# Feed-forward up-projections by seven products of sums of quarters, down-projections in three parts

## The chip, the cores and the metric

The kernel runs on one core of a Trainium2 chip. The metric is the device time of one execution in microseconds. The kernel before takes 1202.05 us (median of three runs, 1201.83 to 1202.29). The engines are TensorE (PE for its matmuls, PEld for its weight loads), VectorE (DVE), ScalarE (ACT), GpSimd (POOL) and SyncE (SP, which issues nearly all loads).

## The reference

One decoder layer over 512 tokens of width 1024, all in float32:

```python
x = x + 0.5 * swiglu(rmsnorm(x, ffn1_norm), ffn1_wgu, ffn1_wdown)
h = rmsnorm(x, mix_norm); z = h @ w_in         # q, k, v, conv, gates
a = sliding_window_attention(q, k, v, sinks) @ attn_proj
c = silu(layernorm(conv(ca * sigmoid(cb)))) @ conv_proj
x = x + (sigmoid(ga) * a + sigmoid(gb) * c) @ w_out
x = x + 0.5 * swiglu(rmsnorm(x, ffn2_norm), ffn2_wgu, ffn2_wdown)
x = x + sigmoid(rmsnorm(x, ple_gate_norm) @ ple_gate_w) * rmsnorm(p @ ple_proj, ple_norm)
# swiglu(h, wgu, wd):  g, u = split(h @ wgu);  (silu(g) * u) @ wd      with 2816 features
# rmsnorm(x, g):       x * rsqrt(mean(x * x) + eps) * g
```

Nearly all of the arithmetic is in the matrix products: the two feed-forwards have 3 x 1024 x 2816 weights each, the rest some ten products of 1024 x 1024.

## The kernel before

Activations lie transposed in SBUF, features on the 128 partitions and the 512 tokens along the free dimension, so x is eight tiles of 128x512 (`x[k]`, KD = 8). A float32 product is made of three matmuls in the reduced-precision type fp32r. Every operand is split into a high part (`hi`, ACT, a copy that rounds) and a low part (`lo`, DVE, source minus high). `mm3` (line 702) then adds lo x hi, hi x hi and hi x lo into one PSUM bank. A matmul has a 128x128 block of weights as its stationary operand and 512 tokens as its moving one.

Weights come in pieces of 128x1024 floats (512 KB): `piece` (line 690) loads one (SP), and splits it. There are three buffers for raw pieces, three for high and three for low parts (`SLOTS`, line 641: raw, hi, lo), 53 tiles of 128x512 for everything else (class a), four tiles four times as wide (class o), two of class k that hold the keys, and the eight PSUM banks (ps).

A feed-forward is the function `ffn` (line 852). Its 22 tiles of features are taken one by one: `products` multiplies the gate and the up part of a tile, 2 x 8 x 3 = 48 matmuls of 512 columns, into two banks. `gated` multiplies both by the norm's factor `rb` (one number per token, spread over the partitions), takes silu of the gate (ACT), the product, and its split. When all 22 are there, eight down-projections follow, each over all 22 tiles (66 matmuls) into one bank, and one DVE instruction adds half of it to `x[o]`. `after(o)` (`next_norm`) makes the next stage's split input and adds its squares on POOL. The factor of a norm is made from sums of columns (`mean_rstd`: eight matmuls of one column, then Newton steps on four numbers per partition) and spread by `spread` (two matmuls with diagonal matrices).

The program isn't written in the order in which it runs. `record` notes all operations; `simulate` lays them on the engines with a table of costs (`costs`), giving each a latest start (`deadlines`), and the order found becomes each engine's queue. TensorE's groups of matmuls may be taken out of order within a window of 8 groups (`WINDOW`). Operations given to `nc.flex` may be put on DVE or on POOL. `ORDER` (line 40) lists the steps of the middle of the layer (convolution, attention, gates), whose steps are not touched otherwise.

All instructions of the program have the line 1348 in the profile, so they are told apart by the names of their tiles: `f_g`, `f_u` and `f_d` are the gate, up and down products of both feed-forwards, `raw_wgu`, `whi_wgu` and `wlo_wgu` a piece of up-projection weights and its halves, `f_gs`, `f_us`, `f_a` the activations, `kvb` the keys' and values' product, `cz` the convolution on DVE, `y` on POOL, `pg` the last gate.

Of the kernel before, what the change touches and what calls it, by code (L numbers as in the profile page):

```python
# [9 lines left out]
F32 = mybir.dt.float32  # L10
F32R = mybir.dt.float32r
I32 = mybir.dt.int32
# [7 lines left out]
D = 1024  # L20
KD = D // P
FF = 2816
KF = KF2 = FF // P
NH = 16
NKV = 2
HD = 64
# [11 lines left out]


ORDER = """  # L40
K0 a0 a2 a1 Q0 A0 b2 b1 b0 a3 A1 E0 E1 b3 A2 E2 a4 V0 A3 a5 E3 V1 b4 Q1 V2 b5
A4 V3 A5 a7 A6 g5 h7 E5 A7 E6 E4 V6 g3 E7 g0 a6 V5 V4 g4 g6 b6 V7 h1 g2 h4 b7
g1 p0 p2 g7 L0 p3 p6 p4 h3 p7 p5 p1 e0 h5 h6 e1 h0 h2
"""
POOLCH = (0, 2, 4)
WARM = 9
MARGIN = 0.0

CAPS = {"cz": 2, "ct": 4}
# [175 lines left out]
class Program:  # L225
    def __init__(self):
        self.ops, self.groups, self.tiles = [], [], []
        self.cur = None
# [15 lines left out]
    def add(self, eng, what, a, k):  # L244
        op = Op()
        op.flex = eng == "FLEX"
        eng = "DVE" if op.flex else eng
        op.i, op.eng, op.home, op.what, op.a, op.k = len(self.ops), eng, eng, what, a, k
        out = [a[0]] if isinstance(a[0], V) else []
        if isinstance(k.get("accum_out"), V):  # L250
            out.append(k["accum_out"])
        if what == "tensor_tensor_reduce":
            out.append(a[7])
        ins = [v for v in a[1:] if isinstance(v, V) and not any(v is o for o in out)]
        ins += [v for n, v in k.items() if isinstance(v, V) and n != "accum_out"]
        op.writes, op.reads = out, ins
        op.preds, op.succs = {}, []
        op.start = op.end = None
        op.done = False
        for vs, w in ((ins, False), (out, True)):  # L260
            for v in vs:
                p0, p1, m, _ = v.region()
                keep = []
                for e in v.vt.log:
                    o, q0, q1, mm, ww = e
                    if (w or ww) and o is not op and p0 <= q1 and q0 <= p1 and m & mm:

                        op.preds[o] = op.preds.get(o, False) or ww
                        if w and p0 <= q0 and q1 <= p1 and not (mm & ~m):
                            continue  # L270
                    keep.append(e)
                v.vt.log = keep
                keep.append((op, p0, p1, m, w))
        for o in op.preds:
            o.succs.append(op)
        op.outs = [v.vt for v in out]
        op.vts = list(dict.fromkeys(v.vt for v in out + ins))
        for vt in op.vts:
            vt.left += 1
        self.costs(op, "POOL" if op.flex else None)  # L280
        op.group = None
        if eng == "PE":
# [101 lines left out]
        op.ls = ls  # L384


WINDOW = 8


def simulate(prog, slots):  # L390
# [253 lines left out]
def record():  # L644
# [19 lines left out]
    ones = nc.tile("ones", [P, P], F32, "c")  # L664
    nc.vector.memset(ones, 1.0)

    nc.scalar.activation(small("table", 1), ones[:, 0:1], AF.Silu)
# [34 lines left out]
    def mm3(ps, w, x, start, stop, first=1):  # L702

        nc.tensor.matmul(ps, w[first], x[0], start=start, stop=False)
        nc.tensor.matmul(ps, w[1 - first], x[0], start=False, stop=False)
        nc.tensor.matmul(ps, w[0], x[1], start=False, stop=stop)

    def part(w, s):
        return w[0][:, s], w[1][:, s]
# [40 lines left out]
    def spread(name, rr):  # L750
# [21 lines left out]
        nc.scalar.copy(rb, ps)  # L772
        return rb

    class SumSq:
        def __init__(self, name):
            self.name, self.accs, self.n = name, [], 0
# [23 lines left out]
    g_all = nc.tile("g_all", [P, 8, KD], F32, "c")  # L801
    nc.scalar.dma_start(g_all, Dram("gains"))
    g_ffn1, g_mix, g_ffn2, g_gate, g_ple, dwb, lng, lnb = (g_all[:, i] for i in range(8))

    x, h = [], []
    ss = SumSq("n1")
# [45 lines left out]
    def ffn(tag, wgu, wdown, h, ss, after, cuts, late, KF):  # L852

        rb = None
        acts = []
        ups = []
        quads = [[nc.tile(f"{tag}_a{q}{p}", [P, 4, S], F32R, "o") for p in "hl"] for q in range(2)]

        def gated(i, pg, pu, rb):
            g = ftile(f"{tag}_gs{i}")  # L860
            nc.vector.tensor_tensor(g, pg, rb, op=ALU.mult)
            nc.scalar.activation(g, g, AF.Silu)
            u = ftile(f"{tag}_us{i}")
            nc.vector.tensor_tensor(u, pu, rb, op=ALU.mult)
            nc.vector.tensor_tensor(u, u, g, op=ALU.mult)
            if i < 8:
                a = [q[:, i % 4] for q in quads[i // 4]]
                split_into(a[0], a[1], u)
                return a
            return split(f"{tag}_a{i}", u)  # L870

        ws, gu = {}, {}

        def products(i, ks):
            if i not in gu:
                gu[i] = ps_tile(f"{tag}_g{i}"), ps_tile(f"{tag}_u{i}")
            for k in ks:
                if k % 4 == 0:
                    ws[i] = piece(wgu, 2 * i + k // 4, cuts=cuts if i < late else 1)
# [12 lines left out]
        for k in range(KD if late else 0):  # L892
            for i in range(late):
                products(i, [k])
        for i in range(KF):
            if i == late and late:
                rb = spread(f"{tag}_n", r)
            if i >= late:
                kn = 2 if i == late and late else KD
                for k0 in range(0, KD, kn):  # L900
                    products(i, range(k0, k0 + kn))
            pg, pu = gu[i]
            if i == max(0, late - 1):
                r = mean_rstd(f"{tag}_n", ss.accs, D)
            if i == late == 0:
                rb = spread(f"{tag}_n", r)
            ups.append((pg, pu))
            pg.vt.late = pu.vt.late = i < late
            for n in range(len(acts), i + 1 if i >= late else 0):
                acts.append(gated(n, *ups[n], rb))  # L910
        for o in range(KD):
            ps = ps_tile(f"{tag}_d{o}")
            with nc.group(f"{tag}_d{o}"):
                for k0 in range(0, KF, 8):
                    kn = min(8, KF - k0)
                    w = piece(wdown, o, n=kn * P, off=k0 * P)
                    for k in range(k0, k0 + kn):
                        mm3(ps, part(w, slice((k - k0) * P, (k - k0 + 1) * P)), acts[k], k == 0, k == KF - 1)
            nc.vector.scalar_tensor_tensor(x[o], ps, 0.5, x[o], op0=ALU.mult, op1=ALU.add)
            after(o)  # L920

    def next_norm(tag, gain):
        h, ss = [], SumSq(f"{tag}_ss")
# [101 lines left out]

    kz = [nc.tile(f"kz{p}", [P, NKV, S], F32R, "k") for p in "hl"]
    for z in kz:
        nc.gpsimd.memset(z.bitcast(F32)[HD:P, 0], 0.0)
        nc.gpsimd.memset(z.bitcast(F32)[0:HD, 1], 0.0)


    vd = [nc.tile(f"v{t}", [P, 2, NKV, 2, HD], F32R, "a") for t in range(NT)]
# [266 lines left out]


    h4, ss4, after4 = next_norm("pg", g_gate)
    ffn("f2", "wgu2", "wd2", h3, ss3, after4, 1, 0, KF2)


    rb4 = None
    for o in range(KD):
        ps = proj(f"pg{o}", "wgate", o, h4)
        if o == 0:
            rb4 = spread("pg", mean_rstd("pg", ss4.accs, D))
        gt = ftile(f"gt{o}")  # L1310
        n = S // 2 if o == KD - 1 else S
        for c in range(0, S, n):
# [135 lines left out]
```

## Time and profile before

| | |
|---|---|
| median of three runs | 1202.05 us |
| the profiled execution | 1202.08 us |
| its span, first to last instruction | 1200.4 us |
| granted TensorE clock | 0.999 |
| busy share: PE, PEld, DVE, ACT, POOL | 99, 82, 61, 42, 27% |
| read from HBM | 112.04 MB, 95 GB/s over the span |
| first feed-forward | to 367 us |
| middle of the layer | 367 to 790 us |
| second feed-forward | 790 to 1150 us |
| last gate | 1150 to 1195 us |

The time is the span and 1.7 us around it. A row of a group reads: line, engine, operation, out<-in, shapes, count, busy us, mean ns of one, idle time of the engine before them and what ended it. A row of a stretch gives its length, the busy us of PE, PEld, DVE, ACT and POOL with counts, the clock, the DMA share and GB/s. Matmuls overlap and their ends are modelled, so their mean duration isn't their price.

### The profile page before, as it was taken

What the parts mean: (1) busy time and instruction counts of PE and PEld (TensorE: products, weight loads), DVE (VectorE), ACT (ScalarE), POOL (GpSimd) and SP (SyncE); (2) the same over time, 40 slices, a digit from 0 to 9 for tenths busy, and PEclk for the clock granted to TensorE, in tenths of its full rate; (3) what the DMA queues carried; (4) which work ended last, traced back from release to release, by engine and by line L of the source; (5) the groups of instructions that cost most, each with busy time, mean ns of one, the idle gap of its engine ahead of it and who ended that gap; (6) DMA issues with size and microseconds to landing.
All of it is one profiled execution on the core that took longest, in us unless ns stands there. A gap on an engine that the chain in (4) does not pass through costs nothing.

```text
span 1200.4 us, 14207 instructions
## 1 busy us (share of the span) xinstructions
PE 1192.4 (99%) x5380; PEld 989.4 (82%) x5380; DVE 731.1 (61%) x1034; ACT 505.3 (42%) x821; POOL 321.3 (27%) x340
## 2 busy tenths in 40 slices
PE   9999999999999999999999999999999999999998
PEld 8888888888888888878888888888888888888886
DVE  6644444444444799998898786665444444444445
ACT  6333233222223669879864673323323332222222
POOL 1000000001111887887987500420000000011110
PEclk9999999999999999999999999999999999999999
DMA  6332323233332321212223222323232323333321
GB/s 223 106 105 88 106 90 103 85 112 97 97 101 88 106 88 54 88 53 71 87 89 106 88 88 92 102 88 105 88 105 88 106 88 100 95 98 97 99 91 71
DMA packets 36069, 115.06 MB, mean 96 GB/s; under 512 B 4512, under 2 KB 7200, under 8 KB 36000
## 3 DMA queue, kind: packets, MB, share of 16 engines
q1 hardware_dynamic: 35856, 114.12, 29.3%
q8 instruction: 42, 0.69, 0.2%
q14 instruction: 27, 0.22, 0.1%
q10 hardware_dynamic: 144, 0.03, 0.0%
HBM read 112.04 MB, written 2.10 MB: 95 GB/s over the span
## 4 chain that ended last, share of the span: by engine, by line
PE 97%; DVE 3%; issue 0%; ACT 0%; POOL 0%; DVEq 0%; POOLq 0%
PE f_g L1348 20%; PE f_u L1348 20%; PE f_d L1348 20%; PE cb L1348 4%; PE gb L1348 4%; PE pg L1348 4%; PE ga L1348 4%; PE cp L1348 4%; PE ap L1348 4%; PE wo L1348 4%; PE ca L1348 3%; PE q0b L1348 2%; PE sc L1348 1%; DVE cz L1348 1%; PE kvb L1348 1%; PE e L1348 1%
## 5 line engine op out<-in xcount | busy, mean ns | idle before, releaser
L1348 ACT ACTIVATE whi_wgu<-raw_wgu 128x1024 fp32r<-128x1024 f32 (+1 forms) x100 | 95.1, 956 | 253.2 <-PE f_u L1348 229.4
L1348 DVE TENSOR_TENSOR wlo_wgu<-raw_wgu,whi_wgu 128x1024 fp32r<-128x1024 f32 (+1 forms) x100 | 110.8, 1113 | 110.7 <-ACT whi_wgu L1348 110.7
L1348 DVE TENSOR_TENSOR wlo_wd<-raw_wd,whi_wd 128x1024 fp32r<-128x1024 f32 (+1 forms) x48 | 65.8, 1371 | 101.4 <-ACT whi_wd L1348 101.4
L1348 ACT ACTIVATE whi_wd<-raw_wd 128x1024 fp32r<-128x1024 f32 (+1 forms) x48 | 47.5, 990 | 174.4 <-PE f_d L1348 112.9
L1348 POOL TENSOR_TENSOR y<-y,ct 128x509 f32<-128x509 f32 (+28 forms) x90 | 114.7, 1298 | 6.7 <-ACT ct L1348 5.0
L1348 DVE SCALAR_TENSOR_TENSOR cz<-u,dww,cz 128x504 f32<-128x504 f32 (+26 forms) x145 | 104.0, 732 | 1.7
L1348 POOL TENSOR_TENSOR pg_ss_sq<-x 128x512 f32<-128x512 f32 x8 | 8.3, 1042 | 338.2 <-DVE x L1348 326.1
L1348 POOL TENSOR_TENSOR mix_ss_sq<-x 128x512 f32<-128x512 f32 x8 | 8.3, 1042 | 329.8 <-DVE x L1348 317.8
L1348 DVE TENSOR_TENSOR f_gs<-f_g,f_n_rb 128x512 f32<-128x512 f32 x44 | 30.3, 691 | 94.4 <-PE f_g L1348 92.9
L1348 PE MATMUL f_d<-f_a_h,wlo_wd 128*128 128x512 f32 x224 | 87.1, 389 | 0.0
L1348 PE MATMUL f_d<-f_a_h,whi_wd 128*128 128x512 f32 x224 | 87.1, 389 | 0.0
L1348 PE MATMUL f_d<-f_a_l,whi_wd 128*128 128x512 f32 x224 | 87.1, 389 | 0.0
L1348 PE MATMUL f_g<-h_h,wlo_wgu 128*128 128x512 f32 x176 | 69.0, 392 | 0.0
L1348 PE MATMUL f_g<-h_h,whi_wgu 128*128 128x512 f32 x176 | 68.9, 391 | 0.0
L1348 PE MATMUL f_g<-h_l,whi_wgu 128*128 128x512 f32 x176 | 68.7, 390 | 0.0
L1348 PE MATMUL f_g<-f_h_h,wlo_wgu 128*128 128x512 f32 x176 | 68.6, 390 | 0.0
L1348 PE MATMUL f_u<-h_h,whi_wgu 128*128 128x512 f32 x176 | 68.5, 389 | 0.0
L1348 PE MATMUL f_g<-f_h_h,whi_wgu 128*128 128x512 f32 x176 | 68.5, 389 | 0.0
L1348 PE MATMUL f_u<-h_h,wlo_wgu 128*128 128x512 f32 x176 | 68.5, 389 | 0.0
L1348 PE MATMUL f_u<-h_l,whi_wgu 128*128 128x512 f32 x176 | 68.5, 389 | 0.0
L1348 PE MATMUL f_u<-f_h_h,wlo_wgu 128*128 128x512 f32 x176 | 68.5, 389 | 0.0
L1348 PE MATMUL f_g<-f_h_l,whi_wgu 128*128 128x512 f32 x176 | 68.5, 389 | 0.0
(403 smaller groups left out, 3145.9 us busy)
## 6 DMA issues: line engine op xcount, KB each, us to landing
raw_wgu<-in_wgu SPq DMA_DIRECT2D x84, 512.0 KB, 3.5
raw_wd<-in_wd SPq DMA_DIRECT2D x32, 512.0 KB, 3.5
raw_wzc<-in_wzc SPq DMA_DIRECT2D x16, 512.0 KB, 3.5
raw_wzg<-in_wzg SPq DMA_DIRECT2D x16, 512.0 KB, 3.4
raw_wd<-in_wd SPq DMA_DIRECT2D x16, 384.0 KB, 3.1
raw_wq<-in_wq SPq DMA_DIRECT2D x8, 512.0 KB, 3.5
raw_wap<-in_wap SPq DMA_DIRECT2D x8, 512.0 KB, 3.5
raw_wcp<-in_wcp SPq DMA_DIRECT2D x8, 512.0 KB, 3.5
```

Of the source, the lines that this page charges most:

```text
L1348: getattr(engines[op.eng], op.what)(*a, **k)
```

## The change

**Pairs.** The first tiles of a feed-forward (four in the first, two in the second: `plain`) are made as before. Every two further tiles are made together by `pair`. The product of two tiles (rows) with 1024 inputs (in two halves) and 512 tokens (in two halves) is a 2x2 by 2x2 product of blocks, and seven products of sums of blocks give it in place of eight. `sums` makes four combinations of the activations' quarters (T) once per feed-forward from x and the gain, on POOL, ACT and DVE, and splits them. `pair` loads four pieces as before (A00, A01, A10 in the raw buffers, A11 in one of class k), forms four sums of them in halves of 512 columns (`add`, eight instructions that may go to DVE or POOL), and splits seven operands instead of four. Each product is 24 matmuls of 256 columns. Products run in blocks of two, (1, 2), (6, 5), (7, 3), and 4 alone; within a block the gate half of both, then the up half. Partial results stay in four banks; ACT and DVE read them in between, in half tiles.

**Three parts.** The features are taken in parts of 8, 8 and 6 tiles. After each, `down` multiplies these tiles alone, with eight groups of 24 (or 18) matmuls, and adds into x each time. The order of weights and their bytes stay.

**Factor at the output.** The up half is no longer multiplied by the norm's factor; each down result is, in its bank, before it is added to x.

**The rest.** The factor of the last norm is made by `wide_rstd`, for all tokens on all partitions: two matmuls with a constant matrix and Newton steps on 128x512 numbers. The planner gets a window of 10 groups, a limit (`AHEAD`) on how early a weight split may take its buffer, dependencies between TensorE and the other engines by whole bank, and operations that are kept behind a given matmul (`behind`): the loads of A11 and the zeroing of the key tiles. `ORDER` has some steps moved. The load of the gains is issued before the instruction that loads ACT's table. Pieces of tiles 2 and 3 of the first feed-forward come in four cuts.

The core of the diff:

```diff
-WINDOW = 8
+WINDOW = 10
...
+            if c in ("hi", "lo") and slack > AHEAD:
+                return False
...
+    def wide_rstd(name, acc):
+        parts = split(f"{name}_a", acc)
+        ps, b = ps_tile(f"{name}_mb"), ps_tile(f"{name}_nb")
+        with nc.group(f"{name}_mb"):
+            for i, part_ in enumerate(parts):
+                nc.tensor.matmul(ps, mean_r, part_, start=i == 0, stop=i == 1)
+        y = ftile(f"{name}_rb")
+        nc.vector.tensor_scalar(y, ps, 1.0, EPS, op0=ALU.mult, op1=ALU.add)
...
+        for _ in range(3):
+            nc.vector.tensor_tensor(b, ps, y, op=ALU.mult)
+            nc.vector.tensor_tensor(b, b, y, op=ALU.mult)
+            nc.vector.scalar_tensor_tensor(y, b, 1.5, y, op0=ALU.add, op1=ALU.mult)
+        return y
...
+    HS = S // 2
+    CH = 8
+    def sums(tag, gain):
+        t1, t2 = slice(0, HS), slice(HS, S)
+        forms = [[] for _ in range(4)]
+        for q in range(KD // 4):
+            vs = [ftile(f"{tag}_t{f}_{q}") for f in range(4)]
+            for j in range(2):
+                k, v = 2 * q + j, [t[:, j * HS : (j + 1) * HS] for t in vs]
+                g1, g2 = gain[:, k : k + 1], gain[:, k + 4 : k + 5]
+                nc.gpsimd.tensor_tensor(v[0], x[k][:, t2], x[k][:, t1], op=ALU.subtract)
+                nc.scalar.activation(v[0], v[0], AF.Copy, scale=g1)
+                nc.scalar.activation(v[2], x[k][:, t2], AF.Copy, scale=g1)
+                for to, xs, less in ((2, t2, 2), (1, t2, 0), (3, t1, 1)):
+                    nc.vector.scalar_tensor_tensor(
+                        v[to], x[k + 4][:, xs], g2, v[less], op0=ALU.mult, op1=ALU.subtract
+                    )
+            for f in range(4):
+                hi, lo = split(f"{tag}_t{f}_{q}", vs[f])
...
+        def pair(i, T, new):
...
+            add(0, A[1, 0], A[1, 1], ALU.add)
+            add(1, sm[0], A[0, 0], ALU.subtract)
+            add(3, A[0, 1], sm[1], ALU.subtract)
+            add(2, A[0, 0], A[1, 0], ALU.subtract)
...
+            def times(m, n, w, b, to, start):
+                with nc.group(f"{tag}_p{n}{i}_{m}"):
+                    for k in range(4):
+                        c = k * 256 + m * P
+                        mm3(to[m], part(w, slice(c, c + P)), b[k], start and k == 0, k == 3, skip=n in (3, 4, 6, 7))
...
+            for m in both(1, A[0, 0], quarter(0, lo_), 2, A[0, 1], quarter(4, lo_), True):
+                to = (g, u)[m][0][:, lo_]
+                nc.scalar.copy(to, b1[m])
+                nc.vector.tensor_tensor(b1[m] if m == 0 and not new else to, b2[m], to, op=ALU.add)
+                if m == 0:
+                    nc.vector.tensor_tensor(to, to if new else b1[m], rb[:, lo_], op=ALU.mult)
+            for m in both(6, sm[1], T[1], 5, sm[0], T[0], False):
+                nc.scalar.copy(U[m][:, lo_], b2[m])
+                nc.scalar.copy(U[m][:, hi_], b1[m])
+            for m in both(7, sm[2], T[2], 3, sm[3], quarter(4, hi_), False):
+                nc.vector.tensor_tensor((g, u)[m][1][:, hi_], b2[m], U[m][:, hi_], op=ALU.add)
...
+            w = form(4, A[1, 1])
+            for m in range(2):
+                times(m, 4, w, T[3], b2, False)
...
+        def down(k0, k1):
+            for o in range(KD):
+                w = piece(wdown, o, n=(k1 - k0) * P, off=k0 * P)
+                ps = ps_tile(f"{tag}_d{k0}_{o}")
+                with nc.group(f"{tag}_d{k0}_{o}"):
+                    for k in range(k0, k1):
+                        mm3(ps, part(w, slice((k - k0) * P, (k - k0 + 1) * P)), acts[k], k == k0, k == k1 - 1)
+                nc.vector.tensor_tensor(ps, ps, rb, op=ALU.mult)
+                nc.vector.scalar_tensor_tensor(x[o], ps, 0.5, x[o], op0=ALU.mult, op1=ALU.add)
...
+        T = sums(tag, gain)
+        for i in range(plain, KF, 2):
+            pair(i, T, i == plain)
+            if (i + 2) % CH == 0 or i + 2 == KF:
+                down((i + 1) // CH * CH, i + 2)
...
-    ffn("f1", "wgu1", "wd1", h, ss, after, 4, 2, KF)
+    ffn("f1", "wgu1", "wd1", h, g_ffn1, ss, after, 4, False, 4)
...
-    ffn("f2", "wgu2", "wd2", h3, ss3, after4, 1, 0, KF2)
+    ffn("f2", "wgu2", "wd2", h3, g_ffn2, ss3, after4, 1, False, 2)
...
-            rb4 = spread("pg", mean_rstd("pg", ss4.accs, D))
+            rb4 = wide_rstd("pg", ss4.accs[0])
```

More of the change, by code (lines that the diff above doesn't have):

```diff
@@ L281, in add @@
         op.group = None
+        if self.behind is not None:
+            op.preds.setdefault(self.behind, False)
+            self.behind.succs.append(op)
         if eng == "PE":
@@ new lines, in record @@
+    CH = 8
[16 more added lines that the diff above has]
+                hi, lo = split(f"{tag}_t{f}_{q}", vs[f])
+                for j in range(2):
+                    forms[f].append((hi[:, j * HS : (j + 1) * HS], lo[:, j * HS : (j + 1) * HS]))
+        return forms
@@ L872, in ffn, with act_split @@
+    def ffn(tag, wgu, wdown, h, gain, ss, after, cuts, wide, plain):
+        rb = None
+        acts, quads = {}, {}
+        def act_split(i, u):
+            c, q = i // CH, i % CH // 4
+            if (c, q) not in quads:
+                quads[c, q] = [nc.tile(f"{tag}_a{c}{q}{p}", [P, 4, S], F32R, "o") for p in "hl"]
+            acts[i] = [t[:, i % 4] for t in quads[c, q]]
+            split_into(acts[i][0], acts[i][1], u)
         ws, gu = {}, {}
@@ L878, in products @@
                 if k % 4 == 0:
[L879 removed]
+                    ws[i] = piece(wgu, 2 * i + k // 4, cuts=cuts)
                 if k == ks[0]:
@@ L911, in ffn, with gated @@
[L911 to L920, printed above, removed]
+        def gated(i):
+            pg, pu = gu[i]
+            g = ftile(f"{tag}_gs{i}")
+            nc.vector.tensor_tensor(g, pg, rb, op=ALU.mult)
+            nc.scalar.activation(g, g, AF.Silu)
+            nc.vector.tensor_tensor(g, pu, g, op=ALU.mult)
+            act_split(i, g)
@@ new lines, in ffn @@
+        first = None
+        for k in range(KD):
+            for i in range(2):
+                products(i, [k])
+                first = first or nc.groups[-1].ops[0]
+        if wide:
+            rb = wide_rstd(f"{tag}_n", ss.accs[0])
+        else:
+            r = mean_rstd(f"{tag}_n", ss.accs, D)
+            rb = spread(f"{tag}_n", r)
+        for i in range(plain):
+            if i > 1:
+                products(i, range(KD))
+            for ps in gu[i]:
+                ps.vt.late = True
+            gated(i)
@@ L1027, in record @@
     for z in kz:
+        nc.behind = next(o for o in reversed(nc.ops) if o.eng == "PE")
         nc.gpsimd.memset(z.bitcast(F32)[HD:P, 0], 0.0)
         nc.gpsimd.memset(z.bitcast(F32)[0:HD, 1], 0.0)
+        nc.behind = None
     vd = [nc.tile(f"v{t}", [P, 2, NKV, 2, HD], F32R, "a") for t in range(NT)]
```

114 lines of the change are left out of this document (69 added, 45 removed).

## The prediction

> **What bounds the kernel now.** I read the page first (busy times, then the 40 slices), then the chain of waits, then the chain in order of time for the pitch of the matmuls.
>
> ```profile
> span 1200.4 us, 14207 instructions
> PE 1192.4 (99%) x5380; PEld 989.4 (82%) x5380; DVE 731.1 (61%) x1034; ACT 505.3 (42%) x821; POOL 321.3 (27%) x340
> ...
> DVE  6644444444444799998898786665444444444445
> ...
> PE 97%; DVE 3%; issue 0%; ACT 0%; POOL 0%; DVEq 0%; POOLq 0%
> PE f_g L1348 20%; PE f_u L1348 20%; PE f_d L1348 20%; PE cb L1348 4%; PE gb L1348 4%; PE pg L1348 4%; PE ga L1348 4%; PE cp L1348 4%; PE ap L1348 4%; PE wo L1348 4%; PE ca L1348 3%; PE q0b L1348 2%; PE sc L1348 1%; DVE cz L1348 1%; PE kvb L1348 1%; PE e L1348 1%
> ```
>
> TensorE sets the end. The up-projections (f_g, f_u) hold 40% of the chain. DVE is at four tenths in the feed-forwards, slices 2 to 12 and 27 to 39, and full only in the middle of the layer. So matmul time taken out of the feed-forwards comes off the end, unless DVE, which must do more there, becomes late.
>
> A busy TensorE is modelled, so the price of a matmul has to come from counts over stretches. Three rows of the chain in order of time (start, length, matmuls), and the tile view of kvb:
>
> ```profile
> 247.15 119.68 PE f_d L1348 x528
> 366.83 11.51 PE kvb L1348 x96
> ...
> 407.43 21.81 PE q0b L1348 x96
> ```
> ```profile
> L1348 PE MATMUL kvb<-wlo_wkv,mix_h_h x32: 283/283/283, 366.9 to 378.1; 128*128 128x256 f32 x32
> ```
>
> A matmul of 512 columns costs 119.68/528 = 0.2267 us. One of 256 columns, with a weight load of its own each time (5380 loads for 5380 matmuls in the first rows), costs 11.51/96 = 0.1199 us, that is 0.529 of the long one. The recorded durations (283 ns) overlap and are not the price.
>
> **The change, part by part.**
>
> *Seven products for eight.* A pair of feature tiles now takes 2x2x8x3 = 96 matmuls of 512 columns: 96 x 0.2267 = 21.76 us. After it takes 7 products x 2 (gate, up) x 4 x 3 = 168 matmuls of 256 columns: 168 x 0.1199 = 20.14 us. So a pair saves 1.62 us. An eighth of the work would be 2.72; 1.10 goes to the short matmuls. The pairs are (22-4)/2 = 9 in the first feed-forward and (22-2)/2 = 10 in the second: 19 x 1.62 = **-30.8 us**. The down-projections keep their 1056 matmuls.
>
> Against this stands a rule. The kvb stretch has a load for every 256-column matmul and still 0.1199 us. The Trainium skill ("TensorE: Matmul & The Clock Gate", Part 3, "The mechanism") says that a weight load overlaps a running matmul only when its row group differs, and under "LDWEIGHTS" that a load takes its columns over 1.2, about 107 ns for 128. As an estimate by that page a 256-column matmul would take 107 + 107 ns, 0.213 us, a pair 35.9 us and the kernel some 268 us slower. The kvb row excludes it, so it gets no chance below.
>
> *More work on DVE, ACT and POOL per pair.* The rows for its price, by groups that keep shapes apart, DVE first, then ACT, then POOL:
>
> ```profile
> L1348 DVE TENSOR_TENSOR wlo_wgu<-raw_wgu,whi_wgu 128x1024 fp32r<-128x1024 f32 x84 | 104.6, 1245 | 110.0 <-ACT whi_wgu L1348 110.0
> L1348 DVE TENSOR_TENSOR f_gs<-f_g,f_n_rb 128x512 f32<-128x512 f32 x44 | 30.3, 691 | 94.4 <-PE f_g L1348 92.9 <-ACT f_n_rb L1348 1.5
> ...
> L1348 DVE SCALAR_TENSOR_TENSOR f_h_l<-x,g_all,f_h_h 128x512 fp32r<-128x512 f32 x8 | 13.2, 1644 | 0.0
> ...
> L1348 DVE SCALAR_TENSOR_TENSOR h_l<-x,g_all,h_h 128x512 fp32r<-128x512 f32 x8 | 6.1, 764 | 4.4 <-ACT h_h L1348 4.3
> ...
> L1348 DVE TENSOR_TENSOR s<-sc,masks 128x256 f32<-128x256 f32 x8 | 2.9, 412 | 0.0
> ```
> ```profile
> L1348 ACT ACTIVATE whi_wgu<-raw_wgu 128x1024 fp32r<-128x1024 f32 x84 | 89.2, 1062 | 252.2 <-PE f_u L1348 229.4 <-issue 22.8
> L1348 ACT ACTIVATE f_gs<-f_gs 128x512 f32<-128x512 f32 x44 | 27.2, 618 | 2.0 <-DVE f_gs L1348 1.9
> ...
> L1348 ACT COPY s<-sc 128x256 f32<-128x256 f32 x24 | 8.2, 368 | 0.2 <-PE sc L1348 0.2
> ```
> ```profile
> L1348 POOL TENSOR_TENSOR wlo_wzg<-raw_wzg,whi_wzg 128x1024 fp32r<-128x1024 f32 x8 | 19.7, 2466 | 9.8 <-ACT whi_wzg L1348 9.8
> ```
>
> One after another DVE starts them closer than they last; from its timeline in the middle of the layer (start, length):
>
> ```profile
> 497.74 1.22 DVE L1348 TENSOR_TENSOR wlo_wzc<-raw_wzc,whi_wzc 128x1024 fp32r<-128x1024 f32 x1
> 498.88 4.60 DVE L1348 SCALAR_TENSOR_TENSOR cz<-u,dww,cz 128x508 f32<-128x508 f32 x7
> ...
> 512.57 0.68 DVE L1348 TENSOR_TENSOR qT_l<-qTp,qT_h 128x512 fp32r<-128x512 f32 x1
> 513.17 0.68 DVE L1348 TENSOR_TENSOR p_l<-pT,p_h 128x512 fp32r<-128x512 f32 x1
> ```
>
> That is 1.14 us for 1024 columns and 0.60 for 512; for 256 I take 0.34, the 0.41 of the group's mean less the same 0.07. Per pair DVE now gets three 1024-column splits (1, 2, 4), eight 512-column split halves (3, 5, 6, 7), three 512-column steps on activations and twelve 256-column ones: 3 x 1.14 + 11 x 0.60 + 12 x 0.34 = 14.1 us. The eight 512-column sums of weight quarters may run on DVE (8 x 0.60 = 4.8) or on POOL (half of 2.47, 1.23 each, 9.9). So DVE is asked for 14.1 to 18.9 us of each 20.1, 70 to 94%. ACT: 3 x 1.06 + 8 x 0.62 + 6 x 0.37 + 4 x 0.62 = 12.8 us, 64%. All of it lies beside the matmuls; if it does not, it costs what TensorE then waits. How TensorE fares at such a load is seen in the middle of the layer (stretch: its length, then busy us of each engine):
>
> ```profile
> 50.00:250.00 200.00, 200.00 (x884) 165.60 (x883) 95.06 (x112) 60.63 (x75) 0.00 (x0) 1.00 0.29 96
> 250.00:367.00 117.00, 117.00 (x519) 96.93 (x518) 49.74 (x41) 28.94 (x34) 18.61 (x13) 1.00 0.34 102
> ...
> 430.00:480.00 50.00, 50.00 (x243) 41.34 (x242) 48.81 (x100) 41.41 (x106) 42.52 (x59) 1.00 0.19 64
> 480.00:530.00 50.00, 48.47 (x230) 39.74 (x229) 47.97 (x79) 38.86 (x73) 42.34 (x52) 1.00 0.23 75
> 530.00:580.00 50.00, 50.00 (x236) 41.45 (x235) 46.54 (x81) 47.93 (x124) 40.45 (x56) 1.00 0.22 74
> ```
>
> With DVE at 143.3 of 150 us TensorE stood 1.53 us, 1.0%; with DVE at 48% it stood nothing. I take the 1.0% for the pairs: 19 x 0.2 = **+3.9 us**. The bounds are 0 and what the rivals give; I take this end because the pair's load is nearer to the middle's than to the old feed-forward's.
>
> *Sums of the activations* (T, once per feed-forward): 12 STT of 256 columns (half of 0.764, 0.38), 8 splits of 512 (0.60): 9.4 us of DVE, and about as much of ACT, beside the unpaired tiles, 43.5 us of matmuls in the first feed-forward and 21.8 in the second, where DVE is otherwise half idle. Block 2 of the first pair wants only half of them, 5.8 us later still. In the second feed-forward x is final only as the tiles begin, so I put **+1 us** there (0 to 4.7, half of the 9.4).
>
> *Down in three parts, factor at the output.* The up tile's multiplication by the factor (0.69, 44 times) goes. Each of 48 partial outputs instead gets one, and 32 more additions into x: 80 x 0.69 = 55 us of DVE, in stretches where it had 49.74 of 117; beside one group of 5.44 us (24 x 0.2267) stand 1.23 + 0.69 + 0.69 = 2.6 us. Hidden. Each part starts on the last pair's activations: from the end of product 4's gate half it is 0.41 + 0.62 + 0.41 + 0.62 + 0.69 = 2.8 us to the last split; product 4's up half (12 x 0.12 = 1.44) and seven eighths of a down group (4.76) stand before its use. Four more such handovers than before: **+1 us** (0 to 4). Loads, bytes and the SP queue stay; twelve more pieces for tiles 2 and 3 of the first feed-forward come at 0.3 DMA share.
>
> *The last norm.* The column sums on TensorE go, and with them a gap behind the next group:
>
> ```profile
> 1155.49 0.79 PE pg_cs L1348 x8
> 1156.27 11.06 PE pg L1348 x48
> 1167.79 27.25 PE pg L1348 x120
> ```
>
> **-0.8 us**. In their place stand a 512-column split and some 14 DVE steps of about 0.7, 10 us, while six free banks give TensorE 6 x 5.44 = 32.6 us of gate products. Hidden; without that cover it would be the 10.
>
> *Order in the middle, zeroing of the key tiles, waits by whole bank.* TensorE's idle there was 1.53 us, so it can win no more; a worse order might lose as much twice. **0** (-1.5 to +3).
>
> Sum: -30.8 - 0.8 + 3.9 + 1 + 1 = -25.7. The profiled execution took 1202.08 us (span 1200.4 and 1.7 around it), 0.03 over the median of the runs, 1202.05: **1176.4 us**.
>
> **The rivals.**
>
> *All of the gain* (chance 0.27): the order hides the new work fully, as in the old feed-forward. 1202.1 - 31.6 = 1170.5. For it: the 0.00 idle at 50 to 250. Against: DVE's load doubles.
>
> *DVE and POOL in each other's way* (0.16). The same STT of 512 columns takes 0.764 us alone and 1.644 where POOL works, while cz, with one input in PSUM, starts every 4.60/7 = 0.66 under a POOL busy 85%. So sums on POOL and DVE's steps with two SBUF inputs queue up: 3 x 1.14 + 11 x 0.60 + 0.34 + 9.9 = 20.3 us if POOL takes all sums, and where only three quarters of the eleven PSUM steps (3.7) fall under them, 21.2. A pair then saves 0.55: 1202.1 - 19 x 0.55 - 0.8 + 2 = 1192.8. Against it: DVE may take sums itself. The Trainium skill ("SBUF — State Buffer", "SBUF: two separate sides") calls this pair of ports an exclusive lock, by which the loser waits out a whole instruction; the 0.764 and 1.644 agree.
>
> *The third weight buffer, slower* (0.09). Three split-weight buffers serve products in twos. The second form of a block gets the buffer that the first one of the block before leaves, 1.44 us before that block's end, and is wanted 1.44 into its own: 2.88 us, of which half a split uses 0.62 + 0.69 = 1.3. Blocks 2 and 3 are so. If one 1.06 on ACT and a DVE split slowed by POOL stand ahead,
>
> ```profile
> 785.29 1.75 DVE L1348 TENSOR_TENSOR wlo_wgu<-raw_wgu,whi_wgu 128x1024 fp32r<-128x1024 f32 x1 [0.45 <-ACT whi_wgu L1348]
> ```
>
> 1.06 + 1.75 = 2.8 us of delay less 1.6 of slack leave TensorE standing 1.2 twice a pair: 2.4 against 1.62 saved, +0.8 x 19 = +15, 1217. From 0.81 us per handover it is slower than before. Against it: most such delays would have to coincide, and the form is wanted half by half.
>
> *It saves no TensorE time* (0.04): short matmuls that change between banks and forms at 0.1295 (21.76/168) instead of 0.1199. About 1202. Only kvb, and the smaller group of scores, speak for the pitch.
>
> **How the numbers follow.** The likeliest is the sum, with 0.44. Its own range is 1171 to 1184: no stalls in the pairs, or the upper ends of T and handovers. The range goes from 1167 (all gain and the middle's best) to 1193 (ports); outside lie the slower cases, 0.13, and a few tails. A change of 0.2%, 2.4 us, is about what a measurement here can tell. Faster 0.44 + 0.27 + 0.16 = 0.87, the same 0.04, slower 0.09.
>
> **What would show it.** The stretch of one pair: 168 matmuls in 20.1 us if the pitch is right, and its TensorE idle gives the stall. DVE's busy share in the pairs should be 75 to 95%; over that, or with POOL's sums next to splits of 1.7 us, the ports decide. Waits of TensorE for split weights of products 5 and 3 would show the buffer. At the first pair of the second feed-forward a wait for T, and at each down part a wait for its last activation, show the smaller terms. The prediction is wrong if the pair's pitch leaves 0.1199 or TensorE idles over 1 us per pair.

## The result and the profile after

The kernel after takes **1184.28 us** (median of four runs, 1182.44 to 1184.87). The kernel before took 1201.94 (1201.53 to 1202.29, four runs). The ratio is 0.9851, with a 95% interval of 0.9834 to 0.9868: faster by 17.7 us. The forecast was 1176, the range 1167 to 1193. The gain came, and 8 us of it did not.

The profiled execution is the shortest of the four, 1182.44 us with a span of 1180.7. Its page (busy times, two of the slices, the shares of the chain, two groups):

```profile
span 1180.7 us, 17926 instructions
...
PE 1166.4 (99%) x6740; PEld 1029.3 (87%) x6740; DVE 984.3 (83%) x1479; ACT 630.2 (53%) x1117; POOL 492.2 (42%) x444
...
DVE  7996799769986898998999786689966997589876
...
POOL 2330442023334896897899600444302241122340
...
PE 87%; DVE 7%; ACT 3%; issue 2%; DMA 1%; SPq 0%; DVEq 0%; ACTq 0%
...
L1498 POOL TENSOR_TENSOR f_s<-raw_wgu,raw_wgu 128x512 f32<-128x512 f32 x42 | 73.9, 1770 | 337.6 <-DVE f_d L1498 164.0
L1498 DVE TENSOR_TENSOR wlo_wgu<-f_s,whi_wgu 128x512 fp32r<-128x512 f32 x152 | 136.3, 931 | 15.3 <-ACT whi_wgu L1498 15.1
```

TensorE still sets the end, but 7% of the chain now runs over DVE (3% before). DVE's digits in the feed-forwards went from 4 to between 5 and 9. Two groups are new. `f_s` are the eight sums of weight quarters of a pair: of the 152 in the program the planner put 94 on POOL (42 of them in this row) and 58 on DVE. `wlo_wgu<-f_s` are the halves of the split of a sum. They take 931 ns on average, where a DVE step of this size took 0.68 us in the kernel before.

The stretches of five pairs (length, then busy us of PE, PEld, DVE, ACT, POOL; clock, DMA share, GB/s):

```profile
157.97:180.43 22.46, 20.68 (x170) 20.27 (x169) 21.52 (x29) 11.63 (x21) 10.23 (x6) 1.00 0.31 100
180.43:202.31 21.88, 20.68 (x171) 20.27 (x170) 21.03 (x30) 11.59 (x21) 8.49 (x5) 1.00 0.31 101
202.31:222.47 20.16, 20.16 (x171) 20.16 (x170) 16.09 (x29) 12.17 (x22) 0.00 (x0) 1.00 0.25 68
933.20:953.60 20.40, 20.40 (x170) 20.23 (x169) 20.33 (x30) 11.39 (x21) 8.84 (x5) 1.00 0.33 108
953.60:973.76 20.16, 20.16 (x170) 20.16 (x169) 19.50 (x27) 11.74 (x21) 9.07 (x5) 1.00 0.31 101
```

An undisturbed pair takes 20.16 us for its 168 matmuls, 0.1200 each, the forecast's pitch. The third row has no sum on POOL and no standing. The first two are the pairs of tiles 10 and 11 and of tiles 12 and 13 of the first feed-forward, as their waits name them; they are 2.3 and 1.7 us longer. The 19 pairs together take 392.0 us, where 19 x 20.155 would be 382.9: **9.1 us of standing**, 7.7 of it in five pairs of the first feed-forward. The fifth row stands for the opposite case: POOL busy for 9 us, and nothing lost. So work on POOL alone does not decide; it matters when it falls.

Where the first of these pairs stood, TensorE's timeline shows (start, length, and in brackets the idle time and who ended it):

```profile
165.05 0.28 PE L1498 MATMUL f_g10b<-f_t_l,whi_wgu 128*128 128x256 f32 x1
166.40 0.39 PE L1498 MATMUL f_g10a<-f_t_h,wlo_wgu 128*128 128x256 f32 x1 [1.07 <-DVE wlo_wgu L1498]
...
168.09 0.39 PE L1498 MATMUL f_g10a<-f_t_h,wlo_wgu 128*128 128x256 f32 x1 [0.71 <-DVE wlo_wgu L1498]
```

The step from 165.05 to 166.40 is 1.35 us instead of 0.12, so TensorE stood 1.23 us; at 168.09 it stood 0.87 more. It waited for the low halves of the second form of block 2 (product 5, whose bank is `f_g10a`), one half at a time. DVE and POOL in the same microseconds:

```profile
162.87 1.79 DVE L1498 TENSOR_TENSOR f_us<-f_us,f_gs 128x512 f32<-128x512 f32 x1
164.58 3.46 DVE L1498 TENSOR_TENSOR wlo_wgu<-f_s,whi_wgu 128x512 fp32r<-128x512 f32 x2
```
```profile
162.27 3.53 POOL L1498 TENSOR_TENSOR f_s<-raw_wgu,raw_wgu 128x512 f32<-128x512 f32 x2 [10.75 <-DMA raw_wgu<-in_wgu]
165.76 1.73 POOL L1498 TENSOR_TENSOR f_s<-f_s,raw_wgu 128x512 f32<-128x512 f32 x1
167.45 1.74 POOL L1498 TENSOR_TENSOR f_s<-raw_wgu,raw_wgu 128x512 f32<-128x512 f32 x1
```

The two split halves took 1.73 us each, and an activation step ahead of them 1.79, while POOL ran one sum after another at 1.73 to 1.76. The same pair of halves in the pair of tiles 10 and 11 of the second feed-forward:

```profile
939.80 1.29 DVE L1498 TENSOR_TENSOR wlo_wgu<-f_s,whi_wgu 128x512 fp32r<-128x512 f32 x2
```

There they took 0.65 us each. So the change's own sums on POOL made its own splits 2.7 times as long, at a place of the pair that has little slack. DVE had no gap ahead of them, and the high parts were ready (ACT, 162.55 to 163.70), so they were not late for want of their sums. Over the whole trace 54 of the 152 split halves overlap a sum on POOL and take 1.38 us on average; the other 98 take 0.68. The buffer of that form comes free when the first form of block 1 has been used, 36 matmuls or 4.32 us after the pair's start, at 162.3; product 5 wants it at 157.97 + 5.76 (block 1, 48 matmuls) + 1.44 (12 of product 6) = 165.17. That is the window of 2.88 us that the prediction's third rival named.

Which waits this made in the whole kernel, by who is waited for (TensorE's weight loads: total us, times, longest):

```profile
PEld f_g10a L1498 <- DVE wlo_wgu L1498: 2.4, 3, 1.3
...
PEld f_g12a L1498 <- DVE wlo_wgu L1498: 1.6, 2, 0.9
...
PEld f_g18a L1498 <- DVE wlo_wgu L1498: 1.1, 2, 0.9
...
PEld f_g16a L1498 <- DVE wlo_wgu L1498: 0.8, 1, 0.8
```

The longest rows of the pairs all have the same form: a low half from DVE. In the pair of tiles 18 and 19 they lie in block 3: the timeline names product 7 there (`f_g18b`, first form) and product 3 (`f_g18a`, second form). No row names an activation of a down part, T, or a DMA of weights.

### The profile page after: what moved, and what is told of

Same layout as the page of the kernel before. It is cut to its first block, busy times and chain, and to the rows that moved or that the text cites. A ratio compares the mean times of both kernels' runs of the same rounds, so it can differ in the third digit from the quotient of the medians.

```text
span 1180.7 us, 17926 instructions
## 1 busy us (share of the span) xinstructions
PE 1166.4 (99%) x6740; PEld 1029.3 (87%) x6740; DVE 984.3 (83%) x1479; ACT 630.2 (53%) x1117; POOL 492.2 (42%) x444
## 4 chain that ended last, share of the span: by engine, by line
PE 87%; DVE 7%; ACT 3%; issue 2%; DMA 1%; SPq 0%; DVEq 0%; ACTq 0%
PE f_d L1498 20%; PE ga L1498 4%; PE ap L1498 4%; PE cp L1498 4%; PE wo L1498 4%; PE cb L1498 3%; PE pg L1498 3%; PE ca L1498 3%; PE gb L1498 2%; DVE wlo_wgu L1498 2%; PE f_g L1498 2%; PE f_u L1498 2%; PE q1b L1498 2%; DVE cz L1498 2%; PE sc L1498 2%
## 5 line engine op out<-in xcount | busy, mean ns | idle before, releaser
L1498 POOL TENSOR_TENSOR f_s<-raw_wgu,raw_wgu 128x512 f32<-128x512 f32 x42 | 73.9, 1770 | 337.6 <-DVE f_d L1498 164.0
L1498 DVE TENSOR_TENSOR wlo_wgu<-f_s,whi_wgu 128x512 fp32r<-128x512 f32 x152 | 136.3, 931 | 15.3 <-ACT whi_wgu L1498 15.1
L1498 ACT ACTIVATE whi_wgu<-f_s 128x512 fp32r<-128x512 f32 x152 | 88.7, 625 | 58.9 <-PE f_d L1498 13.3
L1498 POOL TENSOR_TENSOR y<-y,ct 128x507 f32<-128x507 f32 (+27 forms) x90 | 114.2, 1292 | 5.8 <-ACT ct L1498 4.2
L1498 DVE TENSOR_TENSOR wlo_wgu<-raw_wgu,whi_wgu 128x1024 fp32r<-128x1024 f32 (+1 forms) x93 | 108.4, 1174 | 7.7 <-ACT whi_wgu L1498 7.2
L1498 DVE SCALAR_TENSOR_TENSOR cz<-u,dww,cz 128x510 f32<-128x510 f32 (+25 forms) x145 | 105.0, 734 | 2.5
L1498 DVE TENSOR_TENSOR f_d<-f_d,f_n_rb 128x512 f32<-128x512 f32 x48 | 33.5, 698 | 70.8 <-PE f_d L1498 70.6
L1498 POOL TENSOR_TENSOR f_s<-raw_wgu,f_s 128x512 f32<-128x512 f32 x28 | 46.1, 1650 | 58.0 <-DVE f_us L1498 28.4
L1498 ACT ACTIVATE ct<-u,dww 128x505 f32<-128x505 f32 (+28 forms) x90 | 58.3, 702 | 2.2 <-DVE u L1498 2.1
L1498 POOL TENSOR_TENSOR f_s<-f_s,raw_wgu 128x512 f32<-128x512 f32 x24 | 38.8, 1618 | 18.3 <-DVE f_s L1498 6.0
L1498 DVE TENSOR_TENSOR f_s<-raw_wgu,raw_wgu 128x512 f32<-128x512 f32 x34 | 35.7, 1054 | 0.7 <-DVE f_a10l L1498 0.4
```

The lines of the kernel that those rows point to most:

```text
L1498: getattr(engines[op.eng], op.what)(*a, **k)
```

## The experiments

The theory from the first profile: sums on POOL and DVE steps that read two SBUF operands hold each other up, and the standing of the pairs is only that. Three others were open: the window of the third buffer is too short by itself; DVE at 90% and more makes TensorE wait, wherever the sums run; POOL is a cheaper place for the sums than DVE.

### The same order, all sums on DVE

The order of every queue as the planner found it; only the engine of the sums is set afterwards.

```diff
     prog, _ = plan()
+    import re
+    for op in prog.ops:
+        if op.flex and op.outs and re.match(r"f[12]_s\d_", op.outs[0].name):
+            op.eng = "DVE"
```

> The changed kernel with its order kept as it is, and all 152 sums of weight quarters on DVE (94 of them were on POOL, 1.6 to 1.8 us each). Theory P (ports): TensorE's standing in the pairs (9.2 us in the changed kernel, 7.9 of it in pairs 10, 12, 16 and 18 of the first feed-forward) comes from splits that wait for POOL's sums. Then the split halves of summed weights fall from a mean of 931 ns to about 690, the pairs' standing falls to 2 or 3 us, and the time to about 1178. Rival D (DVE has too much to do, whoever does the sums): DVE takes on 94 x 0.6 = 56 us, the standing stays or grows, and the time is 1184 or more.

**1173.54 us** (1173.14 to 1174.53, four runs), ratio 0.9765 (0.975 to 0.9779). Its groups of splits and of sums, and the stretches of the two pairs shown above:

```profile
L1502 DVE TENSOR_TENSOR wlo_wgu<-f_s,whi_wgu 128x512 fp32r<-128x512 f32 x152 | 99.3, 686 | 14.1 <-ACT whi_wgu L1502 13.5
L1502 DVE TENSOR_TENSOR f_s<-raw_wgu,raw_wgu 128x512 f32<-128x512 f32 x76 | 49.8, 685 | 2.8 <-DMA raw_wgu<-in_wgu 1.8
```
```profile
157.06:177.22 20.16, 20.16 (x170) 20.16 (x169) 19.08 (x35) 11.53 (x21) 0.00 (x0) 1.00 0.32 111
924.39:944.55 20.16, 20.16 (x171) 20.16 (x169) 18.65 (x33) 11.88 (x21) 0.00 (x0) 1.00 0.29 105
```

DVE is busy 19.08 of 20.16 us, 95%, and TensorE does not stand; over all 19 pairs it stands 0.2 us, where the expectation left 2 or 3. (By their rows, four of the pairs in the kernel after stand 7.3 us, not the 7.9 that the expectation gives them.) So DVE's load is not what the pairs paid for. A split half takes 686 ns again. 10.7 us of the kernel's time go away with 94 instructions moved from one engine to the other.

### No sums: POOL writes a constant in their place

Each sum becomes an instruction of POOL that fills its destination with a constant. The sums are left out of the computation; order, buffers and waits stay. The line stands in the same loop.

```diff
+            op.eng, op.what, op.a, op.k = "POOL", "memset", (op.a[0], 0.5), {}
```

> The same order, but each of the 152 sums is replaced by a POOL instruction that only writes a constant into the sum's tile, so sums are left out of the computation, and neither DVE nor the ports see them. Theory P and rival D both expect the pairs' standing under 1 us and about 1175. If it stays near 9 us, the window between the freeing of a split buffer and its use is too short even for undisturbed splits (rival B), and the time stays at 1182 to 1184.

1173.57 us (1173.41 to 1174.11), ratio 0.9765 (0.9749 to 0.9782); the standing of the pairs is 0. The groups of POOL's and DVE's instructions:

```profile
L1502 POOL MEMSET f_s<- 128x512 f32 x152 | 78.9, 526 | 483.0 <-DVE wlo_wgu L1502 273.8
L1502 DVE TENSOR_TENSOR wlo_wgu<-f_s,whi_wgu 128x512 fp32r<-128x512 f32 x152 | 99.0, 687 | 51.8 <-ACT whi_wgu L1502 50.4
```

Two things follow. The window of the third buffer does not cost anything by itself: with undisturbed splits TensorE waits nowhere in the pairs. And the sums on DVE cost nothing that shows, since a kernel without them takes the same time. POOL runs 152 instructions here, each shorter (526 ns), and by the trace 54 split halves overlap one of them, as many as overlapped a sum in the kernel after; yet these 54 take 687 ns like all others. So it is sums that read SBUF on POOL that slow DVE, not instructions that only write.

The Trainium skill ("SBUF — State Buffer", "SBUF: two separate sides") says that a pair of ports is locked for a whole instruction, and that a DVE instruction with two SBUF inputs competes for it only with a GpSimd instruction that reads SBUF. The second half agrees with 0.931 us (94 sums on POOL) and 0.687 us (constants). A lock for the whole instruction agrees less well: the last section has 1.73 us where strict turns would take 1.96.

### The same order, all sums on POOL

The other dose: 152 sums there in place of 94, by the same loop.

```diff
+            op.eng = "POOL"
```

> The changed kernel with its order kept, and all 152 sums on POOL instead of 94. Theory P: the pairs' standing grows with the sums that share the ports, from 9.2 us to 15 or more, and the time to 1190 or more; a split half next to them lasts 1.0 us or more on average. Rival D: DVE is relieved of 58 x 0.6 = 35 us, so the standing falls and the time is 1182 or less.

1190.05 us (1189.4 to 1193.09), ratio 0.9907 (0.989 to 0.9925). Its groups, and the stretches of two pairs of the first feed-forward (tiles 10 and 11, tiles 18 and 19):

```profile
L1502 POOL TENSOR_TENSOR f_s<-raw_wgu,raw_wgu 128x512 f32<-128x512 f32 x76 | 127.6, 1696 | 298.0 <-DVE f_d L1502 101.9
L1502 DVE TENSOR_TENSOR wlo_wgu<-f_s,whi_wgu 128x512 fp32r<-128x512 f32 x152 | 159.4, 1085 | 12.2 <-ACT whi_wgu L1502 11.5
```
```profile
159.76:180.46 20.70, 20.44 (x170) 20.24 (x169) 20.50 (x25) 11.73 (x21) 15.88 (x9) 1.00 0.36 116
288.05:312.32 24.27, 21.77 (x168) 20.55 (x169) 24.24 (x27) 11.53 (x21) 14.30 (x9) 1.00 0.20 69
```

A split half takes 1085 ns on average, and the pairs stand 16.9 us. With 0, 94 and 152 sums on POOL they stood 0.2, 9.1 and 16.9 us, though DVE has fewer instructions the more POOL takes. Pair by pair the dose does not decide: the pair of tiles 10 and 11 falls from 2.3 us to 0.55, that of tiles 18 and 19 rises from 2.2 to 4.1. With the constants, this settles the cause of the pairs' standing as a whole; which pair stands how long depends on when the sums fall.

### Sums on DVE, order worked out anew

Here the planner knows that the sums are DVE's, and makes its own order.

```diff
-                    nc.flex.tensor_tensor(sm[n][c], *ab, op=op)
+                    nc.vector.tensor_tensor(sm[n][c], *ab, op=op)
```

> All sums bound to DVE, with the order worked out anew for that. Theory P: no pair stands more than 0.3 us, 1176 to 1179, though DVE is busy some 95% of a pair. Rival D: DVE becomes the bound in the pairs, TensorE stands 0.5 us or more in most of the 19, and the time is 1186 or more.

1173.88 us (1173.63 to 1175.09), ratio 0.9768 (0.9754 to 0.9783). The expectation was 1176 to 1179. The pairs stand 0.4 us in all. It is not better than the held order: what the pairs no longer lose is all there is to win there. The start of its profiled execution is longer (below).

### Parts, factor and last norm, without the pairs

All 22 tiles are made one by one, down-projections in three parts; no T and no sums. The cuts of tiles 2 and 3 stay.

```diff
-                    ws[i] = piece(wgu, 2 * i + k // 4, cuts=cuts)
+                    ws[i] = piece(wgu, 2 * i + k // 4, cuts=cuts if i < 4 else 1)
...
-        for i in range(plain):
+        for i in range(KF):
...
-        T = sums(tag, gain)
-        for i in range(plain, KF, 2):
-            pair(i, T, i == plain)
-            if (i + 2) % CH == 0 or i + 2 == KF:
-                down((i + 1) // CH * CH, i + 2)
+            if (i + 1) % CH == 0 or i + 1 == KF:
+                down(i // CH * CH, i + 1)
```

> No pairs: all 22 tiles one by one with products of 512 columns, but down in three parts, the factor at the output and the last norm as in the changed kernel. Theory: the three parts and the norm cost what the prediction says, -0.8 and +1, so 1201 to 1203 beside 1202 before. Rival: each of the four further handovers costs TensorE 1 us or more, and the time is 1205 or more.

1203.13 us (1202.91 to 1203.58, ten runs), ratio 1.001 (1.0001 to 1.002). So all else that the change does costs about 1 us in this kernel, and the pairs bring the whole gain. The waits of its weight loads that touch the down parts, of a stretch that holds the end of the first feed-forward:

```profile
PEld f_d L1495 <- DVE f_a21l L1495: 0.4, 1, 0.4
...
PEld f_d L1495 <- ACT f_a21h L1495: 0.3, 1, 0.3
```

Only the last part, at tile 21, waits for its activations; the two new handovers of each feed-forward, at tiles 7 and 15, show none. TensorE's start, the time to the fifth tile, was 52.11 us here and 51.15 before: 1.0 us, without any T. Its waits name the factor of the norm there (`f_u` for `f_n_rb`, 1.0 us), a row that neither the kernel before nor the one after has. In the diff the products of tile 2 are one group now, where the kernel before had a group for every two input tiles; whether that makes the wait was not tried.

### T later, and pieces uncut

In the kernel after the fifth tile begins at 53.45 us, 2.3 later than before. DVE's timeline there:

```profile
18.25 0.50 DVE L1498 SCALAR_TENSOR_TENSOR f_t<-x,g_all,f_t 128x256 f32<-128x256 f32 x1
18.67 1.49 DVE L1498 TENSOR_TENSOR n_acc<-n_acc,n_sq 128x512 f32<-128x512 f32 x2
20.07 0.42 DVE L1498 TENSOR_TENSOR wlo_wgu<-raw_wgu,whi_wgu 128x256 fp32r<-128x256 f32 x1
```

Steps of T (`f_t`) stand between the splits on which the first matmuls wait. Two kernels ask whether it is T or the cuts of tiles 2 and 3. Both have the sums on DVE with a new order. In the first, T of the first feed-forward may not run before 30 us:

```diff
+            for v in vs:
+                v.vt.after = 30.0 if tag == "f1" else 0.0
```

> All sums on DVE, and the activations' combinations T of the first feed-forward not begun before 30 us. Theory S (T delays the start): TensorE's standing in the first 30 us, 7.0 us in the kernel with all sums on DVE beside 3.2 in the kernel before, falls to 4.5 or less, and the time by 1 to 2.5 us to about 1172. Rival C (the four cuts of the pieces of tiles 2 and 3 delay it): the standing stays near 7 and the time at 1173 to 1174.

In the second, T is early again and the pieces of tiles 2 and 3 come whole:

```diff
-                    ws[i] = piece(wgu, 2 * i + k // 4, cuts=cuts)
+                    ws[i] = piece(wgu, 2 * i + k // 4, cuts=cuts if i < 2 else 1)
```

> All sums on DVE, and only the pieces of the first two tiles cut in four, as in the kernel before; T as early as in the changed kernel. Theory S: the standing in the first 30 us stays at 6 or more and the time at 1173 to 1174. Rival C: it falls to 4.5 or less, and the time to about 1172.

With T late: **1172.70 us** (1172.16 to 1172.94), ratio 0.9757 (0.9741 to 0.9772), the shortest median here; all its runs lie under those of the kernel that differs in T alone (1173.63 and up), though the intervals of the ratios overlap. With whole pieces: 1174.62 us (1173.55 to 1175.54), ratio 0.9773 (0.9757 to 0.9788), no better than with cuts. In the first 30 us TensorE began 111 matmuls with T early, 124 with T late and 109 with whole pieces (128 in the kernel before); at 0.2267 us each, the 7.0 us of standing that the expectations start from become about 4.1 with T late and 7.5 with whole pieces, as the theory of T has it (the time with whole pieces lies above the 1173 to 1174 expected). The stretches of the start, first with the sums on DVE alone, then with T late besides:

```profile
0.00:54.89 54.89, 52.53 (x221) 42.80 (x222) 46.81 (x107) 34.80 (x76) 6.58 (x19) 0.97 0.58 186
```
```profile
0.00:51.85 51.85, 50.34 (x220) 41.27 (x221) 42.26 (x97) 33.51 (x72) 6.96 (x19) 1.00 0.62 197
```

The start is 3.0 us shorter with T late. About 1.7 of that is a halved clock (0.97 on average; last section), and the 1.3 that are left are put down to steps of T in the way (the planner's order changes with them, so this is argued). That fits the times of the kernels: against the three executions of the kernel with T early that took 1173.63 to 1174.07, the gain is 0.9 to 1.4 us. With T late the start is still 0.7 us longer than before (51.85 against 51.15). That rest was not taken apart, and that it is the wait of the kernel without pairs is not shown.

### The kernel after once more

A second profile, since three of its four executions took about 2 us more than the profiled one.

> The changed kernel once more, for a second profile: its four executions took 1182.4 and 1184.2 to 1184.9 us, the profiled one being the 1182.4. If the spread comes from TensorE's granted clock, this execution has a mean clock under 1.0 and a longer stretch at half clock while the standing in the pairs is again 9 us; if it comes from the ports, the standing in the pairs is 11 us.

1184.21 us, span 1182.5, mean clock 0.998. Its rows are in the last section: the 1.8 us are nearly all a halved clock behind a wait. The pairs are 10.7 us longer than undisturbed ones, but 1.6 of that is the pair with the halved clock; without it the standing is 9.1 again.

## Why the prediction was right and wrong

**What bounds the kernel, and the pitch: right.** TensorE's time came off the end. 20.155 us per pair against 20.14 forecast make 19 x (21.76 - 20.155) = -30.5 us, against -30.8. The rival by which short matmuls save nothing fell with it.

**The standing of the pairs, +3.9: the step that failed.** The prediction read "1.0%" from the middle of the layer and carried it over "because the pair's load is nearer to the middle's". It measured 9.1: 0.48 us a pair on average, and over 1 us in four of them. Worse than the size, the cause was another: DVE's load does not make TensorE stand. With DVE busy up to 95% of a pair TensorE stood 0.2 us in all 19. The sums' price on DVE was right (18.9 us of DVE work per pair forecast, 19.08 in the stretch shown), and so was the room for it. What failed is that sums were priced as if they could go to POOL at 1.23 us each, beside DVE. On POOL the shortest took 1.29, but the means of its groups are 1.6 to 1.8, and a split half beside them took 0.7 us longer on average (1.38 against 0.68), 1.1 at most.

**The rivals were nearer to it.** The second (DVE and POOL in each other's way) forecast 21.2 us per pair with every sum on POOL; that kernel's pairs took 20.155 + 16.9/19 = 21.04, and the kernel 1190.05 against the rival's 1192.8. That the figures are so close is in part luck: the rival adds up DVE's and POOL's work over a whole pair, while DVE was busy 93% of these pairs and they stood between 0 and 4.1 us. In the kernel after it did not come in full, as the planner left 58 of the 152 on DVE. The third named the place: the second form of a block and its 2.88 us (in one pair the first form of block 3 was late too). Its mechanism holds only together with the second's, as the constants showed: with splits of 0.687 us the window is enough. The two were priced apart, as alternatives; what happened was one mechanism, the ports as its cause and the buffer as its place, at 9.1 us. The first rival (all of the gain, 1170.5) is what the sums on DVE come near to: they took 1173.5, and 1.9 us of the difference is its start (53.05 us to the fifth tile), about 1 the pitch, the last norm's new wait and what standing was left. The forecast's range held because it was made wide enough for the second rival. Its lower end, 1167, does not come out of its own terms: 1170.5 less the 1.5 of the middle is 1169.0.

**T, +1 at the second feed-forward: wrong in place, and right in size by luck.** It cost about 1.3 us, in the first feed-forward, where the prediction had it "beside the unpaired tiles". The cover was there, but not at 12 to 24 us, when TensorE lives from one split to the next; no T was seen to be waited for at the second. The pieces of tiles 2 and 3 were rightly put at nothing; the other 1.0 us of the 2.3 by which the start grew was not forecast.

**Four more handovers, +1: 0.** The new parts at tiles 7 and 15 show no wait in the kernel after or in the one without pairs. The last part's waits for tile 21 (0.4 and 0.3 us above) are in the kernel without pairs alone.

**Last norm, -0.8: right, with a small new wait.** The column sums are gone. From the chain of the kernel after, in order of time:

```profile
1131.04 0.70 DVE f_d L1498
...
1133.08 0.68 DVE x L1498
1133.76 0.83 DVE wlo_wgate L1498
1134.59 0.22 issue
1134.82 1.54 DVE pg_h_l L1498
1136.35 0.04 issue
1136.39 5.97 PE pg L1498 x25
1142.37 0.46 PE pg_mb L1498 x2
1142.83 32.69 PE pg L1498 x144
```

`pg_mb` runs inside the stream of gate products with no gap behind it. But the last split input (`pg_h_l`) is now late, and TensorE stands 0.45 us for it. Ahead of it on the chain stand the last output's multiplication by the factor (`f_d`), the addition into x, a weight split that came between, and `pg_h_l` itself. `pg_h_l` takes about twice the 0.764 us of an undisturbed step of its kind; POOL squares x beside it (`pg_ss_sq`, 1.89 us from 1133.91), as it did in the kernel before, where the step took 1.77. The multiplication was rightly called hidden for all outputs but this one; which of the four would have to go for the wait to vanish was not tried.

**Order in the middle, 0: right.** From the first matmul behind the first feed-forward to the first of the second it takes 422.7 us in both kernels.

The sum with what was measured, against the profiled execution of before: 1202.1 - 30.5 - 0.8 + 9.1 + 2.3 (start) + 0.45 = 1182.6; it took 1182.44. The median lies 1.8 above it; in the one of the longer executions that was profiled, that is the clock.

## What to carry to other kernels

Before an operation goes to GpSimd as spare capacity, ask whether it reads SBUF and which VectorE steps with two SBUF inputs run beside it: here both took 1.7 us where 0.67 and 1.29 were the shortest apart, and VectorE at 95% was the better place. Price rivals that meet at one place together: a short window is harmless at one duration and costs at another. Preparatory work that is "beside" a long stretch has to be kept out of the few microseconds in which the bounding engine has no reserve, by a time before which it may not start; here that brought about 1 us.

## What the runs showed of the hardware

**Two engines nearly alternate.** The tile view of the kernel after gives a group's shortest, median and longest duration in ns, and the first and last start:

```profile
L1498 POOL TENSOR_TENSOR f_s<-raw_wgu,raw_wgu x42: 1287/1740/3414, 44.4 to 1071.7; 128x512 f32<-128x512 f32 x42
...
L1498 DVE TENSOR_TENSOR wlo_wgu<-f_s,whi_wgu x152: 674/686/1794, 55.2 to 1089.7; 128x512 fp32r<-128x512 f32 x152
```

At their shortest a sum takes 1.29 us and a split half 0.67. Back to back beside each other each took about 1.73, so that one of each was done in 1.73 us, little less than the 1.96 that strict turns would take. The median split is untouched, 0.686, and the mean 0.93: the loss comes in bursts, where sums run in a row, and so the mean tells too little. Which part of an instruction keeps the other engine out is not shown.

**The clock halves after short waits.** In the second profile of the kernel after, stretches around the same wait:

```profile
165.00:171.00 6.00, 3.93 (x19) 3.43 (x18) 6.00 (x6) 2.36 (x6) 5.23 (x4) 0.72 0.01 3
167.30:170.70 3.40, 3.19 (x13) 2.90 (x14) 3.40 (x4) 0.68 (x2) 2.93 (x2) 0.50 0.02 5
171.00:174.00 3.00, 3.00 (x27) 3.00 (x26) 2.27 (x4) 1.84 (x5) 1.61 (x1) 1.00 0.20 20
```

and TensorE's timeline in it:

```profile
167.47 0.58 PE L1498 MATMUL f_g10a<-f_t_h,wlo_wgu 128*128 128x256 f32 x1 [2.03 <-DVE wlo_wgu L1498]
```

After an idle time of 2.03 us the granted clock was one half for 3.4 us, from 167.3 to 170.7, and the pair took 24.10 instead of 22.46 us. In the first profile, with waits of 1.23 and 0.87 us at the same place, the clock stayed at 1.00. With the sums on DVE in a new order the same happened at the start, after waits of 0.48, 0.76 and 0.50 us between 19.7 and 23.3, and eight matmuls of a single column that took the 0.9 us behind them:

```profile
24.30:27.70 3.40, 3.40 (x10) 2.63 (x10) 2.96 (x16) 3.40 (x10) 0.00 (x0) 0.50 0.36 115
```

The kernel after had similar waits at its start (before 20.54, 21.80 and 23.33 us) and kept 1.00 there. So waits of 0.5 to 2 us can cost about 1.7 us more, in some executions and not in others of the same kernel. The Trainium skill ("TensorE: Matmul & The Clock Gate", "What's actually happening") gives free-running windows of 3413 ns, and the half clock after at least one idle window. The length of the dip agrees; that a whole window must be idle does not, as the longest idle time was 2.03 us. What share of a window must be idle was not measured, and that the waits cause the dip is argued from their order, not shown by a run that changes them alone.
